# A hybrid decoder block on one core: the feed-forward products by a seven-product block scheme

## The chip, the cores and the metric

The kernel runs on one core of a Trainium2 chip, as one launch. The metric is the device time in microseconds. TensorE (PE) does the matmuls, VectorE (DVE), ScalarE (ACT) and GpSimd (POOL) the elementwise work, SyncE (SP) only issues DMAs; a DMA issued by GpSimd stands in GpSimd's own queue. Each engine works through its instructions in the order in which they stand in the program, and waits at an instruction whose inputs or buffers are not there.

## What is computed

One decoder block for 512 tokens of width 2048, in float32: two token mixers side by side (latent attention and chunked gated linear attention), an output projection, then a SwiGLU feed-forward part of width 5632; both sub-layers are normed before and after and modulated by columns computed from a vector `c`. The part that the change rewrites is, in the reference,

```python
h = rms_norm(x, g_pre_ffn) * (1 + scale) + shift
f = (silu(h @ w_ffn_gate) * (h @ w_ffn_up)) @ w_ffn_down
x = x + gate * rms_norm(f, g_post_ffn)
```

with `h` of 512 x 2048, `w_ffn_gate` and `w_ffn_up` of 2048 x 5632 and `w_ffn_down` of 5632 x 2048. The values `scale`, `shift` and `gate` come from `w_ada` (96 columns of 128 features).

## The kernel before

**A product.** A float32 product is made of three matmuls on exact parts (`mm3`, L213): each operand is split into a rounded high part (type fp32r) and a low rest, and high x high, high x low and low x high are added up in PSUM. So L214, L215 and L216 are the three matmuls of every product.

**Weights.** `load_split` (L191) loads a piece of 1 MB as a tile `wr` [128 x 2048] (4 buffers, SP's queue), and makes in two steps of 1024 columns the high part by an ACT cast (L202) and the low part by a DVE subtraction (L203), in tiles `wh` (8 buffers, that is four pairs of parts). `ada` (L225) loads 1 MB of `w_ada` and reduces it on DVE (L228).

**The mixers** end with the output projection (`out_group`, L835), which goes by halves of the tokens (0 and 1, then 2 and 3). `second_norm` (L795), a generator, is stepped by `advance` between pieces of weights: it norms one tile of 128 tokens, turns it with matmuls against a diagonal matrix (L816), modulates on ACT (L820) and splits into `hT` (L825, L826). The norms of tokens 2 and 3 run beside the first products of the feed-forward part, which take tokens 0 and 1 only.

**The feed-forward part** goes in 11 chunks of 512 features: `up_group` makes gate and up of a chunk (per chunk and matrix 4 pieces of weights, 192 matmuls that stream 512 tokens; the first gate chunk in two halves of 256), `silu_all` and `gated` make the product and its parts, `down_group` multiplies by 512 rows of `w_fd` and adds 16 tiles [128 x 512] to the accumulators (L881 on DVE). Chunk by chunk the down products of the chunk before stand between gate and up. Four columns of `w_ada` are done in each of the chunks 2 to 5. `gate_rows` (L246) is called for the second time before the last `down_group` but one: it turns `gate * g_post` into a row through DRAM (DVE copy L256, POOL DMA L257, four POOL DMAs L260).

**The tail** (from L927) does the last 512 rows of `w_fd` token tile by token tile: `wl` holds their parts, with the low parts subtracted on POOL (16 times L934), then per token tile sums (L949), squares (L951), a product with the gate rows on POOL (L952), the last norm and the store.

The order of the instructions on each engine is set by a list scheduler in the framework that builds the program, from the order of the code, the buffers and priorities; only the mixers have a block `in_order`. So the code's order is the rough order, and buffers say how far an engine's work stands ahead.

## Time and profile before

| | us |
|---|---|
| runs (3) | 2233.36, 2228.1, 2233.39, median 2233.36 |
| profiled execution, span | 2231.3 |
| from 771.8 us on (feed-forward part) | 1459.5 |
| PE busy in the span | 2193.2 |
| DVE, ACT, POOL busy in the span | 1121.5, 667.0, 139.0 |

[...] A busy PE is not PE at its peak: matmuls are pipelined, and the spacing between their starts is what one costs in a row.

### The profile page before, as it was taken

The numbers are of one execution on the slowest core, as the hardware profiler recorded it, in microseconds if no ns is written. First come the engines' busy times: TensorE is split into PE (matmuls) and PEld (weight loads), VectorE is DVE, ScalarE is ACT, GpSimd is POOL, SyncE is SP. The second block draws the span as 40 slices with busy tenths as digits, with TensorE's granted clock in tenths as the row PEclk, the third lists the DMA queues.
The fourth block names the chain that finished last, engine by engine and source line by source line (L and its number), as shares of the span: only waits on it lengthen the run. The fifth ranks groups of instructions, "written<-read, shape, count | busy, mean of one in ns | idle before, by whom it ended". The sixth has DMA issues, their size and how long they took to land.

```text
span 2231.3 us, 24677 instructions
## 1 busy us (share of the span) xinstructions
PE 2193.2 (98%) x10042; PEld 1793.6 (80%) x10042; DVE 1121.5 (50%) x1671; ACT 667.0 (30%) x971; POOL 139.0 (6%) x180
## 2 busy tenths in 40 slices
PE   6999999999999899999999999999999999999998
PEld 5888777777888788888888888888888888888887
DVE  6886686776756953334344443433433333343245
ACT  5434233434324643222122222212222222222222
POOL 0000000011103300000000000000000000000044
PEclk9999999999999999999999999999999999999999
DMA  8883575775655653224242342522222222223242
GB/s 328 302 318 120 174 265 190 265 279 211 225 203 189 255 189 132 95 95 169 95 176 102 120 150 95 189 95 96 98 107 96 94 95 95 95 95 103 105 151 95
DMA packets 58388, 354.08 MB, mean 159 GB/s; under 512 B 7432, under 2 KB 7544, under 8 KB 21665
## 3 DMA queue, kind: packets, MB, share of 16 engines
q1 hardware_dynamic: 48528, 321.28, 40.5%
q0 software_dynamic: 9744, 31.21, 3.7%
q8 instruction: 79, 1.29, 0.2%
q14 instruction: 35, 0.29, 0.0%
q10 hardware_dynamic: 2, 0.01, 0.0%
HBM read 332.00 MB, written 20.46 MB: 158 GB/s over the span
## 4 chain that ended last, share of the span: by engine, by line
PE 85%; issue 9%; DMA 3%; DVE 2%; ACT 1%; POOL 1%; SPq 0%; DVEq 0%; POOLq 0%; ACTq 0%
PE ps L214 26%; PE ps L215 26%; PE ps L216 26%; DMA wr<-w_ada 1%; PE ps L578 1%; PE ps L605 1%; PE ps L577 1%; DVE wr L228 1%; DMA t<-x 1%; PE ps L598 0%; DMA wr<-w_out 0%; PE ps L816 0%; PE ps L725 0%; PE ps L170 0%; DVE lo L203 0%
## 5 line engine op out<-in xcount | busy, mean ns | idle before, releaser
L203 DVE TENSOR_TENSOR lo<-wr,hi 128x1024 fp32r<-128x1024 f32 (+2 forms) x386 | 469.9, 1219 | 740.1 <-ACT hi L202 739.4
L202 ACT CAST hi<-wr 128x1024 fp32r<-128x1024 f32 (+2 forms) x386 | 400.2, 1040 | 1196.6 <-PE ps L215 1126.2
L214 PE MATMUL ps<-t,hi 128*128 128x512 f32 (+1 forms) x1904 | 730.7, 385 | 6.8 <-ACT t L300 2.8
L215 PE MATMUL ps<-t,hi 128*128 128x512 f32 (+1 forms) x1904 | 731.8, 384 | 2.3 <-DVE t L302 2.2
L216 PE MATMUL ps<-t,lo 128*128 128x512 f32 (+1 forms) x1904 | 729.4, 384 | 0.0
L214 PEld LDWEIGHTS ps<-t,hi 128*128 128x128 f32 x1904 | 359.0, 189 | 81.1 <-ACT t L300 3.2
L215 PEld LDWEIGHTS ps<-t,hi 128*128 128x128 f32 x1904 | 359.5, 189 | 73.2 <-DVE t L302 3.2
L216 PEld LDWEIGHTS ps<-t,lo 128*128 128x128 f32 x1904 | 359.3, 189 | 69.2 <-issue 0.2
L214 PE MATMUL ps<-hi,t 128*128 128x512 f32 x1040 | 410.5, 395 | 2.0 <-ACT hi L202 0.9
L215 PE MATMUL ps<-lo,t 128*128 128x512 f32 x1040 | 405.4, 390 | 0.0
L216 PE MATMUL ps<-hi,t 128*128 128x512 f32 x1040 | 404.6, 390 | 0.0
L228 DVE CUSTOM_DVE_ANT_0 wr<-wr,cB 128x2048 f32<-128x2048 f32 x96 | 219.5, 2288 | 52.5 <-DMA wr<-w_ada 52.3
L214 PEld LDWEIGHTS ps<-hi,t 128*128 128x128 f32 x1040 | 195.2, 188 | 44.6 <-ACT hi L202 1.3
L215 PEld LDWEIGHTS ps<-lo,t 128*128 128x128 f32 x1040 | 195.3, 188 | 41.7 <-issue 2.3
L216 PEld LDWEIGHTS ps<-hi,t 128*128 128x128 f32 x1040 | 195.2, 188 | 41.5 <-issue 0.5
L881 DVE TENSOR_TENSOR t<-ps,t 128x512 f32<-128x512 f32 x144 | 99.3, 690 | 160.6 <-PE ps L216 160.6
L257 POOL DMA_DIRECT2D gg<-t x2 | 1.0, 509 | 1353.0 <-DVE t L256 1353.0
L894 DVE TENSOR_TENSOR t<-ps,t 128x512 f32<-128x512 f32 x44 | 29.9, 690 | 13.8 <-PE ps L216 13.1
L887 ACT ACTIVATE t<-ps 128x512 f32<-128x512 f32 x44 | 26.0, 598 | 27.4 <-PE ps L216 25.7
L896 ACT CAST t<-t 128x512 fp32r<-128x512 f32 x44 | 25.0, 620 | 29.7 <-DVE t L894 29.7
L847 POOL TENSOR_TENSOR t<-t,gg 128x512 f32<-128x512 f32 x16 | 25.8, 1632 | 60.5 <-ACT ps L846 60.5
L897 DVE TENSOR_TENSOR t<-t,t 128x512 fp32r<-128x512 f32 x44 | 29.3, 706 | 0.1
(206 smaller groups left out, 1145.0 us busy)
## 6 DMA issues: line engine op xcount, KB each, us to landing
wr<-w_ada SPq DMA_DIRECT2D x96, 1024.0 KB, 4.9
wr<-w_fg SPq DMA_DIRECT2D x48, 1024.0 KB, 4.8
wr<-w_fu SPq DMA_DIRECT2D x44, 1024.0 KB, 4.8
wr<-w_fd SPq DMA_DIRECT2D x44, 1024.0 KB, 4.8
wr<-w_kqvr SPq DMA_DIRECT2D x24, 1024.0 KB, 4.8
...
```

The source lines that it names most:

```text
L202: A.copy(out=hi[:, :n], in_=r)
L203: V.tensor_tensor(out=lo[:, :n], in0=r, in1=hi[:, :n], op=ALU.subtract)
L214: T.matmul(ps, lhsT=a, rhs=c_, start=start, stop=False)
L215: T.matmul(ps, lhsT=a, rhs=d_, start=False, stop=False)
L216: T.matmul(ps, lhsT=b, rhs=c_, start=False, stop=stop)
L228: V.tensor_tensor_reduce(out=raw, in0=raw, in1=cB, scale=1.0, scalar=0.0, op0=ALU.mult, op1=ALU.add, accum_out=adac[:, j:j + 1])
L847: nc.gpsimd.tensor_tensor(out=o, in0=o, in1=ggm[n], op=ALU.mult)
L881: V.tensor_tensor(out=facc[t][n], in0=ps, in1=facc[t][n], op=ALU.add)
L887: A.activation(s, ps, AF.Silu)
L894: V.tensor_tensor(out=s, in0=ps, in1=s, op=ALU.mult)
L896: A.copy(out=hi, in_=s)
L897: V.tensor_tensor(out=lo, in0=s, in1=hi, op=ALU.subtract)
```

## The change

**Seven products in place of eight.** The feed-forward part no longer goes chunk by chunk. A matrix is cut 2 x 2 and seven products of sums of blocks stand for the eight of the plain form (the code names them q1, q2, q5, r7, r6, q4, r3). First come all of gate and up, in 22 blocks of 256 features (`NBLK`): the tokens are cut into 0 to 255 and 256 to 511, the features of `h` into two halves of 1024, the columns into gate and up. A block has two halves (`s`), each with seven products of 24 matmuls that stream 256 tokens (N=256). The sums of weights are made in place in the loaded tiles, two per half on DVE (`vadd`) and two on POOL (`padd`), each [128 x 1024], and then split as before into parts (`wparts`). After the second half nine DVE operations [128 x 512] combine the seven results and make silu(gate) * up.

**Forms.** The sums on the token side are made once from `h` (`first_forms`, `more_forms`: 16 subtractions `minus` and 28 splits `parts` [128 x 512]). For the down projection, `pair_forms` makes seven such forms with their parts from every two blocks and spills 14 tiles of 256 KB to DRAM on POOL's queue.

**Down.** Then the down projection runs in 5 chunks of 1024 features, each with two halves of the columns (`p`), seven products each: 14 splits of 1024 columns, two DVE sums and two POOL sums [128 x 2048], 14 PSUM tiles of 12 matmuls (N=512), each added to an accumulator. The forms come back on SP's queue (28 tiles per chunk). At the last chunk seven operations per token pair combine the accumulators. The last 512 features run as in the tail before.

**Moved.** The last 16 columns of `w_ada` go from the chunks into the mixers. The second `gate_rows` call stands after all down products. Blocks 0 and 1 do q1 and q2, which need tokens 0 and 1 only, ahead of the norms of tokens 2 and 3 (`PRO = 2`). `second_norm` scales the row on DVE and turns it with transposes. Some buffers of the mixers come from the pool `t2k` (62 to 73 tiles), and the scratch of the DMA descriptors is set to 4096 bytes.

```diff
-N_T2 = 62
+N_T2 = 73
+NBLK = DFF // 256
+PRO = 2
...
-        for o in (32, 64, 48):
+        for o in (32, 64, 48, 80):
...
+    def more_forms():
+        s2 = [None] * 4
+        for j in range(4):
+            a11, a21, a22 = h2[0][j], h2[1][j], h2[1][4 + j]
+            s1 = t2()
+            minus(s1, a21, a22)
+            form["s1"][j] = parts(s1)
+            minus(a21, a21, a11)
+            form["s3"][j] = parts(a21)
+            minus(a11, a11, s1)
+            s2[j] = a11
+            form["s2"][j] = parts(a11)
             yield
+        for j in range(4):
+            form["a22"][j] = parts(h2[1][4 + j])
+            a12 = h2[0][4 + j]
+            minus(a12, a12, s2[j])
+            form["s4"][j] = parts(a12)
...
+    def wparts(src):
+        hi, lo = wtile(), wtile()
+        A.copy(out=hi, in_=src)
+        V.tensor_tensor(out=lo, in0=src, in1=hi, op=ALU.subtract)
+        return hi, lo
...
+    def up_product(ps, w, f, s, first, last):
+
+        for kk in range(4):
+            rh = cut(form[f][2 * s + kk // 2], (kk % 2) * 256, 256)
+            for b in range(2):
+                mm3(ps[:, b * 256:(b + 1) * 256], cut(w, kk * 256 + b * P, P), rh,
+                    first and kk + b == 0, last and kk + b == 4)
...
+    def spill_parts(src):
+        made = []
+        for v in parts(src):
+            d = dp.tile([P, 512], F32, name=nm("gd"))
+            dma2(out=d, in_=v.bitcast(F32))
+            made.append(d)
+        return made
...
+    for j in range(NBLK):
+        pss = {}
+        for s in range(2):
+            gr, ur = raw_of(w_fg[j, s]), raw_of(w_fu[j, s])
+            b11, b21, b12, b22 = gr[:, :1024], gr[:, 1024:], ur[:, :1024], ur[:, 1024:]
...
+            vadd(b11, b11, b12)
+            padd(b12, b12, b22)
+            product("q5", "s1", b11, "A")
+            product("r7", "s3", b12, "A")
+            vadd(b11, b11, b22)
+            product("r6", "s2", b11, "B")
+            if s == 1:
+                w_, c22 = t2(), t2()
+                minus(q1, pss["r6"], q1)
+                vadd(w_, pss["r7"], q1)
+                vadd(q1, pss["q5"], q1)
+                vadd(c22, pss["q5"], w_)
+            padd(b11, b11, b21)
+            product("q4", "a22", b11, "B")
...
+    for c_ in range(NBLK // 4):
+        fs = {}
+        for p in range(2):
...
+            b11, b21 = raw_of(w_fd[c_, 0, 2 * p]), raw_of(w_fd[c_, 1, 2 * p])
+            product("q1", "a11", b11)
+            b22, b12 = raw_of(w_fd[c_, 1, 2 * p + 1]), raw_of(w_fd[c_, 0, 2 * p + 1])
+            product("q2", "a12", b21)
+            padd(b11, b11, b12)
+            padd(b12, b12, b22)
+            product("r3", "s4", b22)
+            product("q5", "s1", b11)
+            product("r7", "s3", b12)
+            vadd(b11, b11, b22)
+            product("r6", "s2", b11)
+            vadd(b11, b11, b21)
+            product("q4", "a22", b11)
...
+    ggf = gate_rows(1, [t2() for _ in range(4)])
```

**The order on DVE in the steady part.** In the rows below `wr` is a loaded or summed weight tile, `hi`, `lo` and `wh` are parts of weights, `t` a tile [128 x 512], `ps` a PSUM bank; the bracket lists what the instruction waits for (DMAHW and DMASW are landed DMAs, Activation is ACT, the number behind it is a mark of the build). Before, at the end of a chunk, DVE does splits of weights and the gated product:

```order
L894 TENSOR_TENSOR t_8006<-ps_8288,t_8006 128x512 [waits PE_49]
L897 TENSOR_TENSOR t_8524<-t_8002,t_8523 128x512 [waits Activation_49]
L894 TENSOR_TENSOR t_8008<-ps_8289,t_8008 128x512 [waits PE_49]
L203 TENSOR_TENSOR lo_8611<-wr_8604,hi_8610 128x1024 [waits Activation_49]
L897 TENSOR_TENSOR t_8529<-t_8004,t_8528 128x512 [waits Activation_49]
L897 TENSOR_TENSOR t_8534<-t_8006,t_8533 128x512 [waits Activation_49]
L897 TENSOR_TENSOR t_8539<-t_8008,t_8538 128x512 [waits Activation_49]
L203 TENSOR_TENSOR lo_8665<-wr_8662,hi_8664 128x1024 [waits DMAHW0_49,PE_49,Activation_49]
```

Now, in one half of a block (L905 is the split, L925 `vadd`), the sums stand between the splits, on the same tiles:

```order
L905 TENSOR_TENSOR wh_8797<-wr_8792,wh_8796 128x1024 [waits DMAHW0_49,PE_49,Activation_49]
L925 TENSOR_TENSOR wr_8792<-wr_8792,wr_8794 128x1024 [waits DMAHW1_49,DVE_49]
L905 TENSOR_TENSOR wh_8827<-wr_8792,wh_8826 128x1024 [waits PE_49,Activation_49]
L905 TENSOR_TENSOR wh_8860<-wr_8792,wh_8859 128x1024 [waits PE_49,Activation_49]
L925 TENSOR_TENSOR wr_8792<-wr_8792,wr_8794 128x1024 [waits DVE_49]
L905 TENSOR_TENSOR wh_8888<-wr_8794,wh_8887 128x1024 [waits PE_49,Activation_49]
L905 TENSOR_TENSOR wh_8917<-wr_8792,wh_8916 128x1024 [waits PE_49,Activation_49]
L925 TENSOR_TENSOR t_8854<-ps_8614,t_8824 128x512 [waits PE_49,Activation_49]
```

What moved: a split of a sum now waits for a sum of DVE or of POOL on the same `wr` tile and for the cast between them, where before a split waited for a landed load and a cast alone.

**The order on POOL ahead of the tail.** Before, the gate row's DMAs stand behind the stores `x1d` of the second norm, and the 16 subtractions L934 behind those:

```order
L805 DMA x1d_5124<-t_6027 128x512 [waits DMASW1_49,DVE_49]
L257 DMA gg_14413<-t_14415 16x128 [waits DMASW2_49,DVE_49]
L260 DMA t_14406<-gg_14413 128x512 [waits DMASW2_49,DMASW3_49,PE_49,Activation_49]
L260 DMA t_14407<-gg_14413 128x512 [waits DMASW4_49,PE_49]
L260 DMA t_14408<-gg_14413 128x512 [waits DMASW5_49,PE_49]
L260 DMA t_14409<-gg_14413 128x512 [waits DMASW6_49,PE_49]
L934 TENSOR_TENSOR t_14709<-wr_14706,t_14708 128x512 [waits DMAHW2_49,PE_49,Activation_49]
```

Now they stand behind the last sums of the down projection (L922), with the subtractions as L1084:

```order
L922 TENSOR_TENSOR wr_19160<-wr_19160,wr_19158 128x2048 [waits DMAHW4_49,Pool_49]
L257 DMA gg_19403<-t_19405 16x128 [waits DMASW6_49,DVE_49]
L260 DMA t_19396<-gg_19403 128x512 [waits DMASW7_49,DMASW6_49,PE_49]
L260 DMA t_19397<-gg_19403 128x512 [waits DMASW0_49,PE_49]
L260 DMA t_19398<-gg_19403 128x512 [waits DMASW1_49,PE_49]
L260 DMA t_19399<-gg_19403 128x512 [waits DMASW2_49,PE_49]
L1084 TENSOR_TENSOR t_19431<-wr_19428,t_19430 128x512 [waits DMAHW6_49,PE_49,Activation_49]
```

The store L257 waits for a DVE copy, which stands on DVE behind the last combinations of the accumulators (`q4` of p=1, L836):

```order
L925 TENSOR_TENSOR t_16991<-t_16991,t_16876 128x512 [waits DVE_49]
L925 TENSOR_TENSOR t_17030<-ps_19368,t_17030 128x512 [waits PE_49]
L925 TENSOR_TENSOR t_16914<-t_16914,t_16952 128x512
L836 TENSOR_TENSOR t_17030<-t_17030,t_16952 128x512 [waits DVE_49]
L256 COPY t_19405<-ps_19402 16x128 [waits PE_49]
L1099 TENSOR_TENSOR t_16503<-ps_19503,t_16503 128x512 [waits PE_49]
```

What moved: the gate row and the subtractions behind it, from ahead of the last two groups of down products to behind all down products but the tail's.

## Rows read from the trace of the kernel before

**Rows 1.** The page's first lines: busy time by engine, and the chain by engine.

```profile
PE 2193.2 (98%) x10042; PEld 1793.6 (80%) x10042; DVE 1121.5 (50%) x1671; ACT 667.0 (30%) x971; POOL 139.0 (6%) x180
PE 85%; issue 9%; DMA 3%; DVE 2%; ACT 1%; POOL 1%; SPq 0%; DVEq 0%; POOLq 0%; ACTq 0%
```

**Rows 2.** Windows: start:end, length, busy PE PEld DVE ACT POOL, clock, DMA share, GB/s.

```profile
771.80:2231.30 1459.50, 1448.73 (x6606) 1208.45 (x6604) 568.11 (x708) 363.95 (x461) 55.01 (x48) 1.00 0.33 117
1400.00:2180.00 780.00, 780.00 (x3443) 645.78 (x3442) 276.03 (x295) 182.11 (x204) 25.21 (x21) 1.00 0.31 108
```

**Rows 3.** Timeline of PE: start, duration, instruction; N=512, then N=256.

```profile
1499.89 0.39 PE L214 MATMUL ps<-t,hi 128*128 128x512 f32 x1
...
1512.36 0.39 PE L215 MATMUL ps<-t,hi 128*128 128x512 f32 x1
...
790.07 0.28 PE L216 MATMUL ps<-t,lo 128*128 128x256 f32 x1
...
794.74 0.28 PE L216 MATMUL ps<-t,lo 128*128 128x256 f32 x1
```

**Rows 4.** Timeline of the end: the last matmul and the last store.

```profile
2222.21 0.28 PE L216 MATMUL ps<-t,t 128*128 128x256 f32 x1
...
2225.82 2.32 SPq L960 DMA_DIRECT2D y<-t  x4
```

**Rows 5.** Groups by line and shape, whole span: count, busy us, mean ns, idle before.

```profile
L203 DVE TENSOR_TENSOR lo<-wr,hi 128x1024 fp32r<-128x1024 f32 x358 | 442.2, 1237 | 715.0 <-ACT hi L202 714.6
L202 ACT CAST hi<-wr 128x1024 fp32r<-128x1024 f32 x358 | 376.3, 1054 | 1146.1 <-PE ps L215 1100.2 <-issue 31.5 <-DMA wr<-w_kqvr 13.0
L228 DVE CUSTOM_DVE_ANT_0 wr<-wr,cB 128x2048 f32<-128x2048 f32 x96 | 219.5, 2288 | 52.5 <-DMA wr<-w_ada 52.3
L816 PE MATMUL ps<-t,t 128*128 128x128 f32 x128 | 16.0, 277 | 3.9 <-DVE t L811 3.9
```

**Rows 6.** PE's waits around the second norm of tokens 2 and 3 (timeline), and a window behind them.

```profile
739.24 0.35 PE L816 MATMUL ps<-t,t 128*128 128x128 f32 x1 [1.87 <-DVE t L811]
...
760.16 0.38 PE L816 MATMUL ps<-t,t 128*128 128x128 f32 x1 [2.06 <-DVE t L811]
...
775.43 0.39 PE L214 MATMUL ps<-t,hi 128*128 128x256 f32 x1 [1.90 <-ACT ps L846]
...
776.00:780.00 4.00, 4.00 (x23) 4.00 (x23) 3.59 (x10) 1.54 (x3) 2.70 (x3) 0.61 0.67 213
```

**Rows 7.** Timeline of ACT: the last modulation of tokens 3.

```profile
803.32 5.70 ACT L820 ACTIVATE t<-ps,shcol,scol 128x128 f32<-128x128 f32 x16
```

**Rows 8.** Timeline of DVE: instructions that follow each other without a wait.

```profile
2140.78 0.69 DVE L881 TENSOR_TENSOR t<-ps,t 128x512 f32<-128x512 f32 x1 [2.03 <-PE ps L216]
2141.38 2.83 DVE L897 TENSOR_TENSOR t<-t,t 128x512 fp32r<-128x512 f32 x3
...
2145.72 1.23 DVE L203 TENSOR_TENSOR lo<-wr,hi 128x1024 fp32r<-128x1024 f32 x1 [0.30 <-ACT hi L202]
2146.86 0.69 DVE L881 TENSOR_TENSOR t<-ps,t 128x512 f32<-128x512 f32 x1
```

**Rows 9.** Timeline of DVE and POOL where both work; POOL's L952 min/median/max ns.

```profile
2156.62 2.30 DVE L203 TENSOR_TENSOR lo<-wr,hi 128x1024 fp32r<-128x1024 f32 x1 [1.55 <-ACT hi L202]
2158.85 0.68 DVE L881 TENSOR_TENSOR t<-ps,t 128x512 f32<-128x512 f32 x1
2159.45 1.71 DVE L203 TENSOR_TENSOR lo<-wr,hi 128x1024 fp32r<-128x1024 f32 x1
...
2146.28 17.28 POOL L934 TENSOR_TENSOR t<-wr,t 128x512 fp32r<-128x512 f32 x11 [3.83 <-ACT t L933]
...
L952 POOL TENSOR_TENSOR t<-t,t x17: 721/1292/1757, 2183.1 to 2223.6; 128x512 f32<-128x512 f32 x15, 128x256 f32<-128x256 f32 x2
```

**Rows 10.** Groups: POOL's DMA issues of 256 KB, as the spills would be.

```profile
L805 POOL DMA_DIRECT2D x1d<-t x16 | 8.9, 558 | 12.1 <-DVE t L804 8.0 <-DVE rv L154 2.8 <-DVE t L826 0.5
```

**Rows 11.** Timeline of POOL: the gate row and the first subtractions of the tail.

```profile
2136.37 0.51 POOL L257 DMA_DIRECT2D gg<-t  x1 [1347.20 <-DVE t L256]
2138.97 2.16 POOL L260 DMA_DIRECT2D t<-gg  x4 [2.09 <-ACT t L933]
2141.15 1.30 POOL L934 TENSOR_TENSOR t<-wr,t 128x512 fp32r<-128x512 f32 x1
```

**Rows 12.** Windows: a stretch of the mixers (columns as in rows 2).

```profile
275.00:675.00 400.00, 397.52 (x1852) 302.19 (x1851) 278.77 (x489) 144.06 (x249) 41.22 (x77) 0.98 0.64 232
```

More of the change, by code (lines that the diff above doesn't have):

```diff
@@ L501, in fill_out @@
                 ahead = load_split(w_out[todo[i + 1]], 4, 512)
-            for _ in range(1 + q):
+            for _ in range(2):
                 next(more)
@@ L582, in scores @@
         V.tensor_scalar(mx, mx, -ATT_SCALE, None, op0=ALU.mult)
[L583 removed]
+        pr = t2()
         sumc = small(1, "sum")
@@ L771, in block_kernel @@
     chunks = fill_out()
-    ggm = gate_rows(0, [sm.tile([P, 512], F32, tag=t, name=nm("gg"), bufs=BUFS[t]) for t in ("pr", "pr", "pT", "pT")])
+    ggm = gate_rows(0, [t2() for _ in range(4)])
     with in_order():
@@ L792, in block_kernel @@
     osum = cp.tile([P, 16], F32, name="osum")
-    hT = [(t2(F32R), t2(F32R)) for _ in range(KT)]
     def second_norm(t):
@@ new lines, in parts, with minus, first_forms @@
+    def parts(src):
+        hi, lo = t2(F32R), t2(F32R)
+        A.copy(out=hi, in_=src)
+        V.tensor_tensor(out=lo, in0=src, in1=hi, op=ALU.subtract)
+        return hi, lo
+    def minus(out, a, b):
+        V.tensor_tensor(out=out, in0=a, in1=b, op=ALU.subtract)
+    h2 = [[None] * 8, [None] * 8]
+    form = {n: [None] * 4 for n in ("a11", "a12", "a22", "s1", "s2", "s3", "s4")}
+    def first_forms():
+        for j in range(4):
+            form["a11"][j] = parts(h2[0][j])
+            yield
+        for j in range(4):
+            form["a12"][j] = parts(h2[0][4 + j])
+            yield
@@ new lines, in block_kernel, with wtile, raw_of @@
+        advance(30)
+        norms = itertools.chain(*[second_norm(t) for t in toks], (first_forms, more_forms)[th]())
+    def wtile():
+        return wp.tile([P, 1024], F32R, tag="wh", name=nm("wh"), bufs=8)
+    def wparts(src):
+        hi, lo = wtile(), wtile()
+        A.copy(out=hi, in_=src)
+        V.tensor_tensor(out=lo, in0=src, in1=hi, op=ALU.subtract)
+        return hi, lo
+    def raw_of(src):
+        raw = wp.tile([P, 2048], F32, tag="wr", name=nm("wr"))
+        dma(out=raw, in_=src)
+        return raw
@@ new lines, in block_kernel @@
+    early = []
+    for j in range(PRO):
+        raws = [raw_of(w_fg[j, s]) for s in range(2)]
+        q1, sg = t2(), t2()
+        for f, o in (("a11", 0), ("a12", 1024)):
+            ps = bank("A")
+            for s in range(2):
+                up_product(ps, wparts(raws[s][:, o:o + 1024]), f, s, s == 0, s == 1)
+                advance(2 if j == 0 else 3)
+            if f == "a11":
+                A.copy(out=q1, in_=ps)
+        vadd(sg, ps, q1)
+        A.activation(sg, sg, AF.Silu)
+        early.append((q1, sg))
@@ L925, in block_kernel @@
+    facc = [[acc[n // 2][t % 2][("q2", "r6", "q4", "q5")[2 * (t // 2) + n % 2]] for n in range(4)] for t in range(NT)]
+    ggf = gate_rows(1, [t2() for _ in range(4)])
+    gl = [[[back(d) for d in v] for v in blk] for blk in gd[-1]]
     wl = []
     for n in range(4):
-        raw = wp.tile([P, 2048], F32, tag="wr", name=nm("wr"))
-        dma(out=raw, in_=w_fd[NFC - 1, n])
+        raw = raw_of(w_fl[n])
         row = []
@@ L953, in block_kernel @@
         v = small(1, "v1")
-        V.tensor_reduce(out=v, in_=fsum[:, 4 * t:4 * t + len(parts)], axis=AX.X, op=ALU.add)
+        V.tensor_reduce(out=v, in_=fsum[:, 4 * t:4 * t + len(parts_)], axis=AX.X, op=ALU.add)
         v = rsqrt(v, D)
```

196 lines of the change are left out of this document (110 added, 86 removed).

## The prediction

> **What bounds the kernel now.** I read the page's totals first: PE is busy for 98% of the span and makes 85% of the chain, DVE half, POOL 6% [rows 1]. A total hides stages, so the window of the feed-forward part comes next: from 771.8 us on PE is busy for 1448.7 of 1459.5 us, and from 1400 to 2180 for all of it at clock 1.00, with DVE at 276 of 780 us [rows 2]. Busy is not work done, so I price the matmuls by the spacing of their starts: 55 steps of N=512 between 1499.89 and 1512.36 are 0.2268 us each, 39 steps of N=256 between 790.07 and 794.74 are 0.1197 us [rows 3]. The code counts 384 of N=256 (first gate chunk), 4032 of N=512 for the rest of gate and up, 2112 for down: 384 x 0.1197 + 6144 x 0.2268 = 1439.4 us. The other 20.1 us of the window: 8.8 us from the last matmul (ends 2222.5) to the end of the span [rows 4], some 8.0 us for half of the 128 matmuls L816 [rows 5], and one wait of 1.9 us at 775.4 with a clock of 0.61 in the four us behind it, that is 0.39 x 4 = 1.6 us lost [rows 6]. So it is bound by matmuls, and only fewer of them, or cheaper ones, help; everything else has to stay under PE.
>
> **The gain.** Gate and up become 22 blocks x 2 halves x 7 products x 24 matmuls = 7392 of N=256: 884.8 us. Down becomes 5 x 2 x 7 x 2 x 12 = 1680 of N=512: 381.0 us. The last 512 features keep 192: 43.5 us. Sum 1309.3, so **-130.1 us**. A half-size matmul costs more than half, 0.1197 against 0.1134, which takes 46 us of what 7/8 alone would give. The tail's 8.8 and the 64 transposes stay, taken at the same 8.0: 1326.1 us if nothing waits.
>
> [...]
>
> **The price: seven places where PE can wait.**
>
> *1. Start, +30 (18 to 40).* Ahead of the norms of tokens 2 and 3, PE has blocks 0 and 1 of q1 and q2: 8 x 24 x 0.1197 = 23.0 us. Before, the last modulation of token 3 ended at 809.0 [rows 7], 37 us behind the out-projection; I take 35. Then DVE has 16 `minus` and 20 `parts` at 0.60, nine splits and two sums at 1.14, and three POOL sums stand between: about 42 us until block 0's last product can run, with its own 2.9 us about 80. PE alone would have been there at 23.0 + 10 x 2.87 + transposes, 55. So 25, and about 5 more in block 1.
>
> *2. Gate and up, steady, +32 (0 to 100).* Prices first. In a row DVE needs 1.14 us for [128 x 1024] (2145.72 to 2146.86) and 0.60 for [128 x 512] (2140.78 to 2141.38) [rows 8]. POOL's L952 takes 0.721 us for 256 columns and 1.292 for 512, so 2.23 ns per column more [rows 9]; my estimates for 1024 and 2048 are 2.43 and 4.71 (four times the 512 row would be 5.17). And they don't run side by side: while POOL subtracts, a DVE split takes 2.30 and 1.71 us instead of 1.23 [rows 9]. So I add them. Per pair of blocks: 28 splits and 8 sums x 1.14, 18 combinations and 11 operations of the forms x 0.60 = 58.4 us on DVE, 8 x 2.43 = 19.4 on POOL, together 77.8, against 28 x 24 x 0.1197 = 80.4 us on PE. That would just fit, but it is uneven: a half without combinations has some 17.5 us of it, one with combinations 22, with the forms too 26, against 20.1 on PE, and the eight `wh` tiles let DVE be only about two products (6 us) ahead. Within a half the chain sum, ACT cast, split is serial as well: from the split of r6 to the split of q4 it is 2.43 + 1.05 [rows 5] + 0.4. I take 83.6 per pair, 3.2 more than PE, over 10 pairs. If the lock hides it is 80.4; with the rows' full durations (1.24 for 1.14 and so on) it is 83.4 of work and 88.6 with the same waits; 90 is the bound. The 14 spills per pair cost POOL 14 x 0.56 = 7.8 us [rows 10], which leaves it 53 us free, so nothing; but a spill that waits for its `parts` stands ahead of the next POOL sum, and its delay is the next product's.
>
> *3. Change from gate/up to down, +3:* the last pair has its forms to make before down can pass its first product (0 to 6).
>
> *4. Down, +28 (0 to 60).* Per chunk and p PE has 7 x 24 x 0.2268 = 38.1 us; DVE 14 x 1.14 + 2 x 2.28 + 14 x 0.60 = 28.9, POOL 2 x 4.71 = 9.4, together 38.3: no slack. The split of q2 has to wait for both POOL sums at about 11.9 us behind the group's start, and is wanted at 9.5: 2.4 us in nine groups, and 6.6 in the last one, where the 14 combinations of p=0 stand in DVE's order between q1 and q2.
>
> *5. Clock, +6 (0 to 48).* Of three waits of about 2 us in front of the feed-forward part, one was followed by a clock of 0.61, price 1.6 us [rows 6]. Places 1 to 4 make some 30 such waits; I take the four longest.
>
> *6. Tail, +17 (8 to 25).* The gate row now starts behind the last down product, and POOL's subtractions for the tail behind it. Before, from the store L257 to the first subtraction passed 4.8 us (2136.37 to 2141.15), 1.29 us each from there [rows 9, 11], all ahead of the tail. Now L257 waits for L256, behind the last combinations, about 2 us behind the last product: the 16th part is ready 2 + 4.8 + 16 x 1.29 = 27.4 us behind it, and the first token tile can't end before; unhindered it takes 10.9.
>
> *7. Mixers, +3 (0 to 12).* 16 columns x 2.37 us (2.29 [rows 5] and a short read of its sum) is 38 us of DVE and 16 MB, in a stretch where DVE is busy for 279 of 400 us [rows 12] and PE bounds; the cover is DVE's free 30%. Out of the feed-forward part they take nothing off PE.
>
> Sum of the waits inside the window: 30 + 32 + 3 + 28 + 6 + 17 = 116; 1326.1 + 116 = 1442, against 1459.5: -17.4; with the mixers -14.4, so a span of 2217. The median of the runs stood 2.1 above the span of the profiled execution: **2219 us**, 0.6% faster. Nearly all of the 130 us goes back into waits for DVE and POOL.
>
> **Rivals.** What 0.3% either way (6.7 us) can't be told from no change: 2226.7 to 2240 counts as the same.
>
> A, the forecast, 2219, with its own range 2195 to 2245: chance 0.47.
>
> B, PE-bound: DVE's splits run far enough ahead and POOL's sums hide. For it: POOL and DVE together are under PE in gate and up; the casts have half of ACT free. Then place 1 costs 18, 2 nothing, 3 and 4 eight, 5 two, 6 17: 45 instead of 116, 2148. Against it: 38.3 against 38.1 in down, and splits at 2.30. Chance 0.15.
>
> C, the slower side: sums of DVE and POOL bound both stages. If a split costs its full 1.24 and a POOL sum always delays the split behind it, a pair of blocks takes 88.6 us instead of 83.6 (+50) and a group of down 2 us more (+20): 2289. It decides from 85.7 us per pair on: 2.1 x 10 more than the forecast, and the whole is at 2240. Speaking for it: the 2.30 and 1.71 where POOL's instructions have only 512 columns [rows 9]. Chance 0.17.
>
> D, the clock falls behind nearly each wait: 30 x 1.6 = 48 instead of 6: 2261. For it the 0.61 window, against it the two other waits without. Chance 0.08.
>
> E, the lock is narrower than I took it. Between the two slowed splits DVE's add from PSUM took 0.68 us, as always, with POOL busy [rows 9]. So 14 of 18 combinations per pair and the 14 adds per group of down, which read PSUM, may lie beside POOL: 8.4 us each. Half of places 2 and 4 goes: 2219 - 30 = 2189. Chance 0.13. [...]
>
> **How the numbers follow.** Faster than 2226.7: B, E and 0.30 of A, 0.58; the same: 0.11 of A; slower: C, D and 0.06 of A, 0.31. The range 2150 to 2280 leaves out half of B (0.08) and somewhat over half of C (0.10).
>
> **What would show it.** In the trace after: matmuls of N=256 with starts 0.12 us apart inside a product. Steady pairs of 83 to 84 us with waits of PE that end with DVE's split; 80.4 is B, over 86 is C. Splits of over 2 us beside POOL sums, which last about 2.4 and 4.7 us. In down, groups of 40 to 41 us with a wait in front of the second half of q2. A wait of about 20 us in front of the blocks' first q5, and a first token tile of the tail that ends some 28 us behind the last down product, with POOL's subtractions as the releaser. Wrong it would be if POOL's sums cost other than 2.4 and 4.7, or if the mixers grow by more than 12 us, where nothing of the sum above looks.

## The result

The changed kernel takes 2260.68 us (median of 4 runs, 2255.43 to 2268.26) against 2233.38 of the kernel before beside it: ratio 1.0122, 95% interval 1.0094 to 1.0149. It is slower by 1.2%, where 0.6% faster was forecast. The time lies inside the range, the sign is wrong. The profiled execution spans 2253.7 us, 7.0 below the median (before: 2.1 below); it is the fastest of the four.

The page of the changed kernel, busy time by engine, to be held against [rows 1]:

```profile
PE 2109.3 (94%) x12714; PEld 1851.7 (82%) x12714; DVE 1764.0 (78%) x2095; ACT 907.7 (40%) x1265; POOL 540.4 (24%) x436
```

The matmuls did get cheaper: PE is busy 84 us less, DVE 643 us more, POOL 401 us more. The stages are read from the windows of the changed kernel, cut at the first matmul of a stage (columns as in [rows 2]: start:end, length, busy PE, PEld, DVE, ACT, POOL, clock, DMA share, GB/s; the clock is the granted clock of TensorE, 1.00 its full speed):

```profile
794.60:922.20 127.60, 98.96 (x705) 93.84 (x704) 103.40 (x135) 65.06 (x118) 36.49 (x24) 0.87 0.38 139
922.20:1756.20 834.00, 818.10 (x6722) 813.75 (x6722) 694.43 (x653) 357.03 (x410) 275.50 (x219) 0.99 0.40 147
1756.20:1814.20 58.00, 43.55 (x171) 33.88 (x169) 32.42 (x24) 22.84 (x32) 15.76 (x11) 0.91 0.57 219
1814.20:2139.20 325.00, 310.22 (x1345) 253.89 (x1344) 282.28 (x234) 125.22 (x127) 77.72 (x16) 0.99 0.54 194
2139.20:2184.30 45.10, 40.29 (x169) 32.27 (x169) 44.93 (x45) 19.81 (x27) 12.03 (x2) 0.96 0.33 121
2184.30:2253.70 69.40, 49.57 (x206) 37.18 (x204) 30.45 (x63) 13.68 (x39) 42.95 (x38) 0.89 0.41 149
```

The rows are: the first two blocks of gate and up, the other ten pairs, the first group of down, groups 2 to 9, group 10, the tail. Everything up to the first row is the mixers. Against the prediction, clock included:

| stage | matmuls alone | measured | lost | predicted |
|---|---|---|---|---|
| mixers (before: to 771.8) | | to 794.6 | +22.8 | +3 |
| first two blocks | 80.4 + 8.0 | 127.6 | 39.2 | 30 |
| ten pairs | 804 | 834.0 | 30 | 32 + 3 |
| down, group 1 | 38.1 | 58.0 | 19.9 | 2.4 |
| down, groups 2 to 9 | 304.8 | 325.0 | 20.2 | 19.2 |
| down, group 10 | 38.1 | 45.1 | 7.0 | 6.6 |
| tail, to the last matmul (2245.2) | 43.5 | 60.9 | 17.4 | 17 |
| clock | | | some 26, in the rows above | 6 |

The feed-forward part takes 1459.1 us, as before (1459.5, [rows 2]): the whole gain of 130 us is given back inside it. What makes the kernel slower is ahead of it, in the mixers, which the prediction had dismissed with +3.

The clock's share stands inside the rows of the table. Over the feed-forward part the granted clock is 0.97. In the stretches where it is 0.50 the matmuls of N=256 start 0.214 us apart, not 0.120, and those of N=512 0.428, not 0.227. The first row below is the whole part, the second lies in such a stretch; the third, from PE's timeline, is a wait shortly ahead of that stretch, which ended with DVE's split:

```profile
794.60:2253.70 1459.10, 1360.69 (x9310) 1264.80 (x9308) 1187.91 (x1148) 603.64 (x752) 460.44 (x308) 0.97 0.44 159
1106.00:1108.00 2.00, 2.00 (x11) 2.00 (x11) 2.00 (x4) 0.87 (x1) 0.89 (x2) 0.50 0.85 248
1104.56 0.39 PE L216 MATMUL ps<-t,wh 128*128 128x256 f32 x1 [1.01 <-DVE wh L905]
```

At 0.50 PE was busy for 58 us of this part. With the spacings at 0.50 and at 1.00 that makes an estimate of 26 us lost: 9.5 in the first two blocks, 6 in the ten pairs, 4 in the first group of down, 7 in the rest. It does not come per wait: in d_tied (below) PE waits 29 us in the ten pairs and the clock of that window is 1.00.

### The profile page after: what moved, and what is told of

Same layout as the page of the kernel before. It is cut to its first block, busy times and chain, and to the rows that moved or that the text cites. A ratio compares the mean times of both kernels' runs of the same rounds, so it can differ in the third digit from the quotient of the medians.

```text
span 2253.7 us, 32197 instructions
## 1 busy us (share of the span) xinstructions
PE 2109.3 (94%) x12714; PEld 1851.7 (82%) x12714; DVE 1764.0 (78%) x2095; ACT 907.7 (40%) x1265; POOL 540.4 (24%) x436
## 5 line engine op out<-in xcount | busy, mean ns | idle before, releaser
L905 DVE TENSOR_TENSOR wh<-wr,wh 128x1024 fp32r<-128x1024 f32 x448 | 677.8, 1524 | 214.7 <-ACT wh L904 210.3
L904 ACT CAST wh<-wr 128x1024 fp32r<-128x1024 f32 x448 | 464.6, 1050 | 649.0 <-PE ps L215 247.1
L214 PE MATMUL ps<-t,wh 128*128 128x256 f32 x2464 | 705.1, 286 | 18.8 <-ACT wh L904 9.0
L216 PE MATMUL ps<-t,wh 128*128 128x256 f32 x2464 | 704.9, 286 | 12.1 <-DVE wh L905 11.9
L215 PE MATMUL ps<-t,wh 128*128 128x256 f32 x2464 | 703.6, 286 | 4.4 <-DVE t L832 4.4
L214 PEld LDWEIGHTS ps<-t,wh 128*128 128x128 f32 x2464 | 479.0, 194 | 22.5 <-ACT wh L904 11.4
L216 PEld LDWEIGHTS ps<-t,wh 128*128 128x128 f32 x2464 | 478.7, 194 | 15.5 <-DVE wh L905 15.2
L215 PEld LDWEIGHTS ps<-t,wh 128*128 128x128 f32 x2464 | 479.0, 194 | 5.8 <-DVE t L832 5.7
L922 POOL TENSOR_TENSOR wr<-wr 128x1024 f32<-128x1024 f32 x88 | 223.5, 2540 | 500.5 <-DVE wh L905 232.1
L228 DVE CUSTOM_DVE_ANT_0 wr<-wr,cB 128x2048 f32<-128x2048 f32 x96 | 219.2, 2285 | 41.1 <-DMA wr<-w_ada 41.0
L215 PE MATMUL ps<-wh,t 128*128 128x512 f32 x560 | 222.9, 398 | 22.1 <-DVE wh L905 22.1
L214 PE MATMUL ps<-wh,t 128*128 128x512 f32 x560 | 221.4, 396 | 11.4 <-DMA t<-gd 11.3
L216 PE MATMUL ps<-wh,t 128*128 128x512 f32 x560 | 219.9, 395 | 0.5 <-DMA t<-gd 0.5
L215 PE MATMUL ps<-t,hi 128*128 128x512 f32 x432 | 173.0, 400 | 3.1 <-DVE t L302 3.0
L922 POOL TENSOR_TENSOR wr<-wr,wr 128x2048 f32<-128x2048 f32 x20 | 102.6, 5129 | 303.1 <-DVE wh L905 198.7
L216 PE MATMUL ps<-t,lo 128*128 128x512 f32 x432 | 170.4, 395 | 0.0
L214 PE MATMUL ps<-t,hi 128*128 128x512 f32 x432 | 168.7, 398 | 1.3 <-ACT t L300 1.3
L214 PE MATMUL ps<-hi,t 128*128 128x512 f32 x400 | 161.4, 404 | 1.0 <-DVE t L209 0.9
L925 DVE TENSOR_TENSOR wr<-wr,wr 128x1024 f32<-128x1024 f32 (+1 forms) x108 | 153.3, 1420 | 5.5 <-DMA wr<-w_fu 3.2
L215 PE MATMUL ps<-lo,t 128*128 128x512 f32 x400 | 156.6, 392 | 0.3 <-DVE lo L203 0.3
```

What stands on the lines that cost most here:

```text
L214: T.matmul(ps, lhsT=a, rhs=c_, start=start, stop=False)
L215: T.matmul(ps, lhsT=a, rhs=d_, start=False, stop=False)
L216: T.matmul(ps, lhsT=b, rhs=c_, start=False, stop=stop)
L228: V.tensor_tensor_reduce(out=raw, in0=raw, in1=cB, scale=1.0, scalar=0.0, op0=ALU.mult, op1=ALU.add, accum_out=adac[:, j:j + 1])
L904: A.copy(out=hi, in_=src)
L905: V.tensor_tensor(out=lo, in0=src, in1=hi, op=ALU.subtract)
```

## Where the mixers lose: a reordered queue

The mixers lose their 23 us almost wholly in one place. Windows of the kernel before and, in the second row, of the changed one:

```profile
500.00:560.00 60.00, 59.82 (x275) 43.54 (x273) 36.10 (x76) 27.48 (x48) 10.63 (x20) 0.89 0.60 222
```

```profile
500.00:580.00 80.00, 57.14 (x206) 37.26 (x206) 46.30 (x88) 33.83 (x56) 12.81 (x24) 0.74 0.58 205
```

PE is idle for 23 of 80 us, with the clock at 0.74. Its timeline in the changed kernel names the releasers (in brackets: idle before, releaser):

```profile
544.44 0.45 PE L598 MATMUL ps<-cs,t 128*128 128x128 f32 x1 [6.97 <-DVE rc L587]
553.78 0.80 PE L605 MATMUL ps<-t,t 128*128 128x128 f32 x2 [8.89 <-DVE t L681]
```

L598 and L605 are the attention's transposes and value products; L681 belongs to the other mixer (GLA). What L605 reads is the copy L600, which ended at the same moment as L681 (553.72 and 553.73). The two mixers share only queues. ACT's timeline at that place:

```profile
552.38 0.63 ACT L676 ACTIVATE t<-t 128x512 f32<-128x512 f32 x1 [6.33 <-DVE t L674]
552.92 0.56 ACT L585 ACTIVATE t<-ps,mx 128x384 f32<-128x384 f32 x1
...
553.47 0.25 ACT L600 COPY t<-ps 128x128 f32<-128x128 f32 x1
```

ACT stands at a GLA exponential (L676) that waits for DVE, and the softmax step L585 and the copy L600 that PE needs stand behind it; DVE in turn works through columns of `w_ada` (L228, 2.29 us each, and the wait for their loads) ahead of L674:

```profile
548.84 2.29 DVE L228 CUSTOM_DVE_ANT_0 wr<-wr,cB 128x2048 f32<-128x2048 f32 x1 [1.84 <-DMA wr<-w_ada]
```

Two edits could have made this: the 16 columns, or the attention's tiles, which now come from the pool `t2k`. Four runs here and a_ada below tell.

**b_ada**: the kernel before with the columns moved.

```diff
-        for o in (32, 64, 48):
+        for o in (32, 64, 48, 80):
...
-                for _ in range(3):
+                for _ in range(4):
                     next(more)
...
-            for _ in range(1 + q):
+            for _ in range(2):
                 next(more)
```

> The kernel before with one part of the change alone: the last 16 columns of w_ada move from the feed-forward chunks into the mixers (four instead of three per step, two instead of one or two in the output projection). Theory M (these columns make the mixers longer: 38 us of DVE work and 16 MB in front of the short steps of the attention in DVE's order): the feed-forward part starts near 795 instead of 771.8, PE waits of 15 to 20 us at the softmax between 500 and 580, whole 2250 to 2256. Rival P (the attention's tiles from the large pool and the smaller descriptor scratch reorder the mixers): feed-forward part from 772, whole 2233. Forecast of the prediction: +3.

2254.9 us, ratio 1.0087 (1.0066 to 1.0109). The feed-forward part starts at 794.7. The time is what theory M expected, but its place is not: between 500 and 580 us PE is busy for 77.9 of 80 us. The largest part of the waits (PE idle for 8 of 100 us) lies between 300 and 400 us.

**b_pool**: the kernel before with the shared pool (the first gate rows come from it too, and the descriptor scratch is 4096, as in the changed kernel).

```diff
-        pr = sm.tile([P, 512], F32, tag="pr", name=nm("pr"), bufs=BUFS["pr"])
+        pr = t2()
...
-        pT = sm.tile([P, 512], F32, tag="pT", name=nm("pT"), bufs=BUFS["pT"])
+        pT = t2()
...
-N_T2 = 62
+N_T2 = 73
```

> The kernel before with the other part alone that touches the mixers: the attention's tiles pr and pT and the first gate rows come from the pool t2k with 73 tiles, descriptor scratch 4096. Theory M: feed-forward part from 772, whole 2233. Rival P: from near 795, whole 2250 to 2256. Both parts half each: 2244 in both runs.

2250.55 us, 1.0072 (1.0048 to 1.0097); the start is at 791.1. Theory P as well, and with the very wait of the changed kernel:

```profile
544.99 0.80 PE L605 MATMUL ps<-t,t 128*128 128x128 f32 x2 [9.68 <-DVE t L681]
```

Each edit alone costs about what both cost together, so a sum of parts does not describe it.

**a_sm**: the changed kernel with own pools for `pr` and `pT` (and the first gate rows) again, the columns staying in the mixers.

```diff
-        pr = t2()
+        pr = sm.tile([P, 512], F32, tag="pr", name=nm("pr"), bufs=3)
...
-        pT = t2()
+        pT = sm.tile([P, 512], F32, tag="pT", name=nm("pT"), bufs=2)
...
-N_T2 = 73
+N_T2 = 68
```

> The changed kernel with one thing undone: the attention's tiles come from pools of their own again (3 and 2 tiles, t2k at 68). GpSimd's sums, the columns in the mixers and the tail stay. Theory P2 (with the shared pool the scheduler puts a GLA exponential ahead of the last softmax steps on ACT, and PE waits some 25 us for it; the columns alone hide): the feed-forward part starts at 766 to 774 instead of 794.6, the rest as in the changed kernel, whole 2230 to 2240. Rival M2 (the columns make the mixers longer when GpSimd has its part): start at 785 or more, whole 2250 to 2262.

2231.17 us, 0.9995 (0.9975 to 1.0015): start at 773.3, the rest as in the changed kernel. Theory P2: with own pools 21.3 of the 22.8 us are gone. That does not price the columns at the 1.5 us that are left. a_ada keeps the shared pool and takes the 16 columns out of the mixers: it starts at 786.3, 8.3 us earlier than the changed kernel, with the same wait in front of L605:

```profile
540.61 0.79 PE L605 MATMUL ps<-t,t 128*128 128x128 f32 x2 [9.45 <-DVE t L681]
```

So the shared pool makes the wait, with or without the 16 columns; what the columns add depends on the order, from 8.3 us beside the shared pool to nothing that shows with own pools (768.1 with them in f_sm, 769.1 without in f_both), and 22.9 in b_ada. The order of ACT's instructions says how the pool does it. In the changed kernel:

```
L676 ACTIVATE t_3954<-t_3954 128x512
L585 ACTIVATE t_3981,sum_3982<-ps_3974,mx_3978 128x384
L600 COPY t_3989<-ps_3987 128x128
L585 ACTIVATE t_4000,sum_4001<-ps_3993,mx_3997 128x512
L600 COPY t_4009<-ps_4006 128x256
```

and in a_sm:

```
L585 ACTIVATE pr_4000,sum_4001<-ps_3993,mx_3997 128x512
L600 COPY pT_4106<-ps_4102 128x384
L600 COPY pT_4116<-ps_4111 128x512
L676 ACTIVATE t_3954<-t_3954 128x512
```

With pools of their own the first exponential of GLA stands behind the last softmax step; with the shared pool it stands ahead of two of them and four copies. The traces of all runs with the shared pool have it ahead of softmax steps, those of all runs with own pools behind the last one. a_sm changes the number of tiles too (73 to 68), so sharing was not varied quite alone.

**b_ada68**: b_ada with the sizes of a_sm.

```diff
-N_T2 = 62
+N_T2 = 68
...
-    nc = bacc.Bacc("TRN2", target_bir_lowering=False, num_devices=1)
+    nc = bacc.Bacc("TRN2", target_bir_lowering=False, num_devices=1, dynamic_dma_scratch_size=4096)
```

> b_ada (the kernel before with the 16 columns in the mixers) with t2k at 68 instead of 62 tiles and the descriptor scratch at 4096, the sizes that f_sm has. Theory R (with 62 tiles the mixers run short of tiles when the columns come earlier; the room of 68 is what hides the columns in f_sm): feed-forward part from 766 to 776 instead of 798, whole 2226 to 2236. Rival N (the new second norm hides them, or the order is another by chance): from 790 or more, whole 2250 to 2258.

2242.33 us, 1.0049 (1.0032 to 1.0065): start at 782.8, between both theories. Six tiles more and the smaller scratch together take half of the 23 us away. The other half stays open: a_sm has the same columns, own pools and 68 tiles, and starts at 773.3; what is left between them is the new second norm and the buffers that it frees. Which of these it is was not tried.

## Where the feed-forward part loses: sums on GpSimd

**a_dve**: the changed kernel with all sums of weights on DVE.

```diff
     def padd(out, a, b):
-        nc.gpsimd.tensor_tensor(out=out, in0=a, in1=b, op=ALU.add)
+        V.tensor_tensor(out=out, in0=a, in1=b, op=ALU.add)
```

> The changed kernel with all sums of weights on DVE (the 88 sums of 1024 columns and 20 of 2048 leave GpSimd). Theory L (POOL's sums of 2.5 and 5.1 us exclude DVE's splits, so DVE loses more than it is spared): splits fall from a mean of 1.52 to 1.24 us, DVE needs 44 x 1.14 + 29 x 0.60 = 67.6 us per pair of blocks against PE's 80.4, pairs at 80.4 to 81.5 instead of 83.4, -20 to -30; groups of down 33.5 of DVE against 38.1, -5 to -15; whole 2215 to 2235. Rival D (DVE is the scarce engine, 78% busy, and every operation given to it delays a split): pairs above 84, whole above 2265.

2192.57 us, 0.9808 of the kernel before (0.9788 to 0.9829), 68 us less than the changed kernel, more than either theory had. Its windows for the ten pairs and for groups 2 to 9 of down:

```profile
916.10:1722.50 806.40, 806.40 (x6722) 806.40 (x6721) 694.27 (x730) 363.33 (x410) 75.39 (x140) 1.00 0.41 153
...
1775.20:2079.90 304.70, 304.70 (x1346) 252.38 (x1345) 263.66 (x250) 125.35 (x128) 0.00 (x0) 1.00 0.58 207
```

PE never waits now: 80.64 us per pair, 38.08 per group, clock 1.00. The DVE column is the lesson. In the pairs it is busy for 694.3 us with all sums, and was for 694.4 with half of them on GpSimd, though those 80 sums cost DVE 98 us (1.22 each). Giving them away saved DVE nothing: its splits and subtractions took that much longer, and a page of the profile counts the longer duration as busy. The groups of DVE between 1000 and 1400 us, changed kernel first, then a_dve (count, busy us, mean ns):

```profile
L905 DVE TENSOR_TENSOR wh<-wr,wh 128x1024 fp32r<-128x1024 f32 x134 | 195.1, 1467 | 62.5 <-ACT wh L904 61.7
L925 DVE TENSOR_TENSOR t<-ps,t 128x512 f32<-128x512 f32 x49 | 32.7, 684 | 2.0 <-PE ps L216 1.4
L925 DVE TENSOR_TENSOR wr<-wr,wr 128x1024 f32<-128x1024 f32 x39 | 47.7, 1223 | 0.8
L836 DVE TENSOR_TENSOR t<-t,t 128x512 f32<-128x512 f32 x20 | 24.8, 1240 | 0.3
L836 DVE TENSOR_TENSOR t<-ps,t 128x512 f32<-128x512 f32 x20 | 13.7, 684 | 0.0
```

```profile
L905 DVE TENSOR_TENSOR wh<-wr,wh 128x1024 fp32r<-128x1024 f32 x139 | 168.4, 1221 | 48.9 <-ACT wh L904 48.0
L836 DVE TENSOR_TENSOR t<-t,t 128x512 f32<-128x512 f32 x20 | 13.7, 686 | 0.2
```

What stretches has two inputs in SBUF (L905, and L836 on `t,t` to 1240 ns); operations with one input in PSUM keep their 684 ns (40 of the 141 in the ten pairs lie beside a GpSimd sum in time, and all take 0.68 to 0.69 us). Not each one with two inputs in SBUF stretches: DVE's own sums (L925 on `wr,wr`) keep 1223 ns, and none of the 79 in the ten pairs lies beside a GpSimd sum. Of 281 splits there 50 lie beside one: 39 of these take over 2 us, the longest 3.28; the other 11, and the 231 with no sum beside them, take at most 1.3. In down, where a GpSimd sum is 2048 wide, the timelines of DVE and POOL in the changed kernel show two splits that last until such a sum has ended:

```profile
1853.46 8.60 DVE L905 TENSOR_TENSOR wh<-wr,wh 128x1024 fp32r<-128x1024 f32 x2 [2.80 <-ACT wh L904]
```

```profile
1850.79 10.18 POOL L922 TENSOR_TENSOR wr<-wr,wr 128x2048 f32<-128x2048 f32 x2 [29.38 <-DVE wh L905]
```

Two splits, 1.22 us each elsewhere, take 3.03 and 5.64, together 8.60; the first ends 1.1 us behind the first of these two sums (1856.49 against 1855.41), the second 1.1 us behind the other (1862.06 against 1860.97).

This could still be the serial chain: a sum takes 2.5 us on GpSimd and 1.22 on DVE, and cast, split and product wait for it. So the GpSimd work was put back without its place in the chain.

**d_idle**: a_dve with four sums per block on GpSimd, on a tile of zeros that nothing reads.

```diff
+    def idle_sum():
+        nc.gpsimd.tensor_tensor(out=scr, in0=scr, in1=scr, op=ALU.add)
```

> The run a_dve (all sums of weights on DVE, 2193) with four GpSimd sums of 1024 columns per block on a tile of zeros of its own that nothing reads and that waits for nothing: the GpSimd work of the changed kernel's gate and up without its place in the chain. Theory L (GpSimd's sums exclude DVE's splits and sums while they run): splits beside them stretch to 2 to 3.6 us, work per pair of blocks 67.6 + 8 x 2.4 = 87 against PE's 80.6, so pairs above 81.5 up to 87, whole 2205 to 2260. Rival S (only the serial chain sum, cast, split through the slower engine cost the time; the engines run side by side): pairs stay at 80.64, whole 2193.

2301.11 us, 1.0296 (1.0279 to 1.0313), but not by either theory: with nothing to hold them the scheduler put all 88 sums at the start, between 3.6 and 249.7 us. Gate and up kept 80.64 per pair, and the feed-forward part began at 903 instead of 796. So the run says nothing of gate and up. It shows that 239 us of GpSimd work at the start, which no other work waits for, go with a stretch longer by 107 us: in its first 250 us DVE is busy for 230.1 us with 162 instructions, where in a_dve it did 317 in 184.9. (For the tile of zeros `t2k` has 71 tiles here, not 73.)

**d_tied**: the same, with each two sums held in their block by a read of one column of a tile of that block (`t2k` has 70 tiles).

```diff
+    def idle_sums(t):
+        nc.gpsimd.tensor_tensor(out=scr[:, 0:1], in0=t[:, 0:1], in1=zero, op=ALU.mult)
+        for _ in range(2):
+            nc.gpsimd.tensor_tensor(out=scr, in0=scr, in1=scr, op=ALU.add)
```

> a_dve with four GpSimd sums of 1024 columns per block on a tile of its own that nothing reads, held in their block by a read of one column of that block's tile (d_idle had them all run ahead of the feed-forward part). Theory L: GpSimd's sums and DVE's operations on SBUF exclude each other; 67.6 + 8 x 2.4 = 87 us of both per pair of blocks against PE's 80.64: DVE's splits beside them stretch, pairs at 81.5 to 87, whole 2203 to 2260. Rival S: pairs stay at 80.64, whole 2193, as only the serial chain through the slower engine cost the time.

2248.28 us, 1.0060 (1.0035 to 1.0086): 56 us more than a_dve. Every pair takes 84.86 us instead of 80.64, 42 us in ten pairs, though no product waits for these sums; the rest lies in stages ahead of and behind them (the start at 804.1 instead of 796.4, first blocks 126.3 for 119.7, first group of down 56.8 for 52.5). The window of the ten pairs:

```profile
930.40:1779.00 848.60, 819.19 (x6722) 809.02 (x6721) 784.63 (x730) 359.59 (x410) 310.34 (x261) 1.00 0.40 145
```

DVE's 730 instructions are those of a_dve and take 784.6 us, not 694.3. Beside one of the sums DVE's timeline shows

```profile
1016.69 2.76 DVE L905 TENSOR_TENSOR wh<-wr,wh 128x1024 fp32r<-128x1024 f32 x1
1019.38 2.38 DVE L1022 TENSOR_TENSOR t<-t,t 128x512 f32<-128x512 f32 x1
```

where POOL had

```profile
1016.46 4.75 POOL L935 TENSOR_TENSOR scr<-scr 128x1024 f32<-128x1024 f32 x2
```

So the stretching of theory L comes without the chain too, and rival S (the chain alone) is out for gate and up. The sum by exclusion, 67.6 + 19.4 = 87 per pair, was only a bound: 84.86 came. How the changed kernel's own loss in gate and up divides between stretched instructions and chain is not shown, and for down, where d_tied has no sums, the two were not separated.

## The other places

**e_back**: a_dve with four of the first chunk's forms read back ahead of the first weights of down on SP's queue.

```diff
         fs = {}
+        if c_ == 0:
+            for f in ("a11", "a12", "s4", "s1"):
+                fs[f] = [[back(d) for d in gd[q][f]] for q in range(2)]
```

> a_dve with the first chunk's forms a11, a12, s4 and s1 read back ahead of the first weights of the down projection on SP's queue, not behind them. Theory Q (the read-backs of the first group stand in SP's queue behind weight loads that wait for a free weight tile): the first group falls from 52.7 to 38 to 42 us, -10 to -14, whole 2178 to 2184. Rival W (the spills of the last pair are what lands late): first group stays at 50 to 53, whole 2193.

2187.97 us, 0.9793 (0.9775 to 0.9810). The first group falls from 52.5 to 45.7 us, half of what theory Q had. In the changed kernel that group was 58.0. PE's largest waits in it end with read-backs, and SP's queue between 1740 and 1820 us waited (each row: who <- for whom: us in total, times, longest):

```profile
PE ps L214 <- DMA t<-gd: 11.3, 2, 6.5
SPq L910 <- DVE wr L925: 30.6, 2, 18.8
SPq L910 <- DVE wh L905: 17.2, 3, 15.1
```

L910 are the weight loads, which wait for a free tile; the read-backs stand behind them. 45.7 - 38.1 = 7.6 us are left, 5.1 of them waits for other read-backs; their cause was not looked for.

**e_tail**: a_dve with the gate row ahead of the down projection and the tail's 16 subtractions on DVE, two edits at once.

```diff
-    ggf = gate_rows(1, [t2() for _ in range(4)])
...
+    ggf = gate_rows(1, [t2() for _ in range(4)])
     acc = [[{} for _ in range(2)] for _ in range(2)]
...
-            nc.gpsimd.tensor_tensor(out=lo, in0=r, in1=hi, op=ALU.subtract)
+            V.tensor_tensor(out=lo, in0=r, in1=hi, op=ALU.subtract)
```

> a_dve with the second gate row made ahead of the down projection, and the 16 subtractions of the last 512 features on DVE instead of GpSimd (0.60 instead of 1.29 us). Theory T (the tail waits for GpSimd's subtractions, which stand behind the gate row): the tail falls from 61.4 us to 44 to 50 against 43.5 of matmuls, whole 2179 to 2187. Rival: the tail waits for the loads or for free tiles, and stays above 57: 2190 and more.

2185.13 us, 0.9777 (0.9759 to 0.9795). The tail falls from 61.4 to 47.2 us, as theory T said; some 5 of the 14 us went again in stages that the edit doesn't name (the start at 798.1 instead of 796.4, first blocks 120.9 for 119.7, first group 54.1 for 52.5). The chain it removed, on POOL in the changed kernel:

```profile
2187.47 0.51 POOL L257 DMA_DIRECT2D gg<-t  x1 [31.50 <-DVE t L256]
2189.62 2.17 POOL L260 DMA_DIRECT2D t<-gg  x4 [1.64 <-issue]
2191.80 19.85 POOL L1084 TENSOR_TENSOR t<-wr,t 128x512 fp32r<-128x512 f32 x16
```

The last down product started at 2184.1; the 16th part was ready 27.6 us behind it, against 27.4 in the prediction.

**e_pro**: a_dve with four early blocks.

```diff
-PRO = 2
+PRO = 4
```

> a_dve with four instead of two blocks whose first two products run ahead of the norms of tokens 2 and 3 (23 us more of PE work there). Theory F (PE waits at the start only because the forms of tokens 2 and 3 come late; the 31 us that the first blocks lose beside their own 88 are waiting): 12 to 23 us less, whole 2170 to 2181. Rival G (DVE is what is late there, and the eight added splits come in front of the forms): 0 to -8, whole 2185 to 2193.

2195.36 us, 0.9828 (0.9806 to 0.9850): no gain. The first two blocks take 119.5 instead of 119.7 us, the next two 83.2 instead of 80.6. Theory F is out; the time lies just above the range of rival G. For DVE being late speaks that it was busy for 19.57 of 20 us between 850 and 870 in a_dve. In e_pro itself PE's longest waits there (16.4 us) end with ACT's copies of the early products (L937), which stand in ACT's queue among casts (L831) that wait for DVE.

**a_ada**: the changed kernel with one column of `w_ada` in each of the blocks 4 to 19, not in the mixers.

```diff
+        if 4 <= j < 20:
+            ada(76 + j)
```

> The changed kernel with the 16 columns taken out of the mixers again, one in each of blocks 4 to 19 of gate and up. Theory M: feed-forward part from about 772 instead of 794.6; the columns cost 2.4 us of DVE per block in a stage where pairs of blocks are at 82.8 to 84.2 with PE 80.4, so 0 to 3 us per pair, 0 to 24 in all: whole 2238 to 2262. Rival P: feed-forward part still from 794, whole 2260 to 2284.

2333.03 us, 1.0432 (1.0406 to 1.0459), far outside what was expected: pairs with two columns take 92 to 95 us and the pair ahead of them 88. The feed-forward part starts at 786.3, between the two theories. **f_ada** is the same edit on a_dve with the edits of e_back and e_tail.

> a_dve with the tail of e_tail, the read-back of e_back, and the 16 columns of w_ada in blocks 4 to 19 of gate and up instead of the mixers. If the 72 us that this move cost in a_ada came from DVE's load (2.4 us more per block on an engine that GpSimd shut out), gate and up stays near 80.64 per pair now and the feed-forward part starts near 786: 2165 to 2172. If it came from the weight tiles (each column takes one of four, and the weights behind it land later), pairs stay near 90: 2240 and more.

2207.81 us, 0.9884 (0.9853 to 0.9916); start at 787.4, pairs at 83.5 to 86.7, between the two forecasts. So the price has two parts. Without GpSimd's sums a column costs 2.35 us over the ten pairs (844.0 against 806.4), beside them 5.1 (915.7 against 834.0): more than half of it came with GpSimd's sums. For the rest, SP's queue in a_ada between 1000 and 1400 us waits with the weights behind a column:

```profile
SPq L910 <- DVE adac L228: 98.3, 8, 13.8
```

and DVE's sums wait 25.7 us for landing weights, where in a_dve they waited 0.7 us (groups by line of the same stretch, a_ada first):

```profile
L925 DVE TENSOR_TENSOR wr<-wr,wr 128x1024 f32<-128x1024 f32 x34 | 41.4, 1218 | 25.7 <-DMA wr<-w_fu 25.7
```

```profile
L925 DVE TENSOR_TENSOR wr<-wr,wr 128x1024 f32<-128x1024 f32 x40 | 48.9, 1222 | 0.7
```

A column takes one of the four weight tiles, and the load behind it waits for its reduction. That this makes the price is not shown: in f_ada the queue waits as long behind columns (94.4 us), DVE's sums 13.9 us for weights, and the 2.35 us are no more than the reduction itself takes (2.29). A tile of its own for the columns was not tried.

## A version that beats both

**f_sm**: a_dve with the edits of e_back and e_tail, and the attention's tiles in pools of their own (the three diffs of e_back, e_tail and a_sm on top of that of a_dve).

> a_dve with the tail of e_tail and the read-back of e_back, and the attention's tiles in pools of their own again (3 and 2 tiles, t2k at 68). If the shared pool made the mixers longer (b_pool), the feed-forward part starts at 772 to 785 instead of 797; if the 16 columns alone are enough for it (b_ada), at 793 to 800. Whole 2155 to 2180.

2152.02 us, ratio 0.9641 (0.9609 to 0.9673): 3.6% faster than the kernel before, a little below the range. The feed-forward part starts at 768.1, its ten pairs take 80.64 us each and its tail 47.2. First blocks (119.5) and first group of down (50.6) still lose 31 and 12.5 us.

**f_both** adds the diff of a_ada to it, which moves the columns out of the mixers.

> f_ada and f_sm together: the mixers as in the kernel before. Feed-forward part from 770 to 776 if these two parts of the change are all that made the mixers longer; from 785 or more if something else (the new second norm) does. Whole, if the columns hide in gate and up: 2148 to 2158.

2187.65 us, 0.9795 (0.9768 to 0.9822), 30 us above the forecast. It starts at 769.1, no earlier than f_sm, and its pairs cost 83.5 to 87.1: once the attention has its own tiles, the columns cost nothing that shows in the mixers, and 38 us in gate and up.

## Why the prediction was wrong

- **What bounds, and the gain.** Right. The steps of 0.1197 and 0.2268 us [rows 3] hold: where PE doesn't wait, a pair takes 80.64 us (80.4 worked out) and a group 38.08 (38.1).
- **Place 7, the mixers: the step that failed.** +3 was forecast, at most 12; +22.8 came, the sign of being wrong that the prediction itself had named. It priced the 16 columns alone. It put the other edit in the mixers, that `pr` and `pT` move to the shared pool, at nothing and gave no reason, though the diff shows it. A pool moves no work, but it moved the order on ACT: without it 21.3 us are gone (a_sm), and the kernel is level with the one before (0.9995). The comparison of the orders was made for gate and up, POOL and the tail, not for ACT in the mixers. The cover for the columns, DVE's free 30%, held only in part: with the order of own pools they hide, beside the shared pool they add 8.3 us, and in the kernel before 22.9.
- **Place 4, down: the second step.** The first group lost 19.9 us instead of 2.4: that the read-backs stand behind weight loads on SP's queue was left out. Of the loss, 5.5 us go with the sums on GpSimd (a_dve), and 6.8 more with the order on that queue alone (e_back); the rest, the clock in it, stays open. A queue that a step is put on needs the same look as an engine. Groups 2 to 10 came as worked out (20.2 for 19.2 and 7.0 for 6.6), with POOL's sums at 5.13 us on average, not 4.71, and groups of 39.5 to 43.3 us, not 40 to 41.
- **Place 5, clock.** 6 was forecast, the estimate from the rows is 26, inside the rows of the other places. That is half the way to rival D (48). Its whole, 2261, is what came, but by another sum: that it met the time is luck.
- **Place 1, start.** 39.2 against 30, inside the bound; without the 9.5 of the clock it is 30. The one wait of 20 us did not come: PE's 28.6 us of waiting are in pieces, the longest 5.7. With the sums on DVE the start is 31.3, so some 8 us go with GpSimd's sums.
- **Place 2, gate and up.** 30 us lost against 32 + 3, pairs at 82.8 to 84.2 against 83.6. What the prediction calls the lock was its reading of three rows [rows 9]. That DVE's work stretches beside such sums is shown (d_tied, 784.6 us for 694.3), but the 3.2 us were taken between 0 and 8.2, not worked out, and 6 of the 30 are the clock: that the number fits this well is partly luck. POOL's sums took 2.54 us, not 2.43. Of the rivals, B did not come (no pair at 80.4, splits of up to 3.28 us); C would have needed pairs above 85.7. E's condition holds, operations on PSUM keep their 684 ns beside a sum too, but the pairs lost their 3 us all the same.
- **Place 6, tail.** Right, 17.4 against 17, by the chain as written.
- **The sum.** 2217 was forecast for the span, 2253.7 came: 19.8 more from the mixers, 17.5 from the first group of down, 9 from the start, less 5 from places 2 and 3 and less 6 for the clock, which lies inside the other rows. The mixers' miss turns no change into a slower kernel; for the forecast gain the first group would have had to hold as well. The median stood 7.0 above the span, not 2.1: 5 us more, as the profiled execution was the fastest.

The forecast's weakest point was its shape: 116 us of waits against 130 of gain leaves a difference of 14, and an error of that size in one term turns the sign.
